# A hybrid decoder layer on one core: three adaLN sections summed on VectorE instead of in TensorE blocks, HGRN2's key copies put later, and the last down tile in two column halves

## The chip, the cores and the metric

The kernel runs on one core of a Trainium2 chip. The metric is the device time of one execution in microseconds (us). The engines are named as in the profile: PE is TensorE's matrix multiplication and PEld its weight load, DVE is VectorE, ACT is ScalarE, POOL is GpSimd, SP is SyncE, which issues nearly all DMAs of this kernel. `L12` is line 12 of the kernel before.

## What is computed

One layer: 512 tokens of width 1024, everything in fp32. A small vector `c` gives, through a weight matrix `w_ada` of 1024 x 6144, six modulation vectors ("adaLN sections") of width 1024 each: shift, scale and gate for the first sub-layer (sections 0 to 2) and for the second (3 to 5). Cut to what matters here:

```python
cs = silu(c)                                  # (1, 1024)
mod = cs @ w_ada + b_ada                      # (1, 6 * 1024)
sh1, sc1, gt1, sh2, sc2, gt2 = split(mod, 6)

h  = rmsnorm(x, norm1_g) * (1 + sc1) + sh1
z  = h @ w_in                                 # split into the inputs of two head groups
o  = concat(hgrn2(...), nsa(...))             # gated linear recurrence | sparse attention
x  = x + gt1 * (o @ w_out)

h2 = rmsnorm(x, norm2_g) * (1 + sc2) + sh2
u  = causal_dwconv(h2 @ w_up)                 # width 3
a, v = split(u, 2)
x  = x + gt2 * ((silu(a) * v) @ w_down)       # w_down is 2816 x 1024
```

`hgrn2` is a recurrence over four heads of width 128 with gates between 0 and 1; `nsa` has eight query heads of width 64 and three branches (compressed, selected, window).

## The kernel before

**Tiles.** Tokens are cut into four row tiles of 128. The large products (`w_in`, `w_out`, `w_up`, `w_down`) are made of three fp32r matmuls each (`mm3`, L137 to L139): every operand is split into a high part (ACT cast, L133) and a remainder (DVE subtraction, L134). Weights come by DMA into `raw` (two buffers, issued by `issue`, L206 to L211), are split into `whi` and `wlo` and used one part ahead (`piece`, `next_parts`).

**Order.** The order of instructions on each engine is the order in which the code writes them. Where several pieces of work run side by side, they are generators, and `emit` (L147) takes turns: it always advances the one that has gone the smallest share of its given number of yields. So the number beside a generator sets how it is spread. The stages in order are:

1. adaLN sections 0 and 1 and the first projection (to about 60 us);
2. `proj_kv` beside `prep(PREP1)`, then `proj_a` beside `prep(PREP2)`: projections on PE, norms and rotary embedding of queries and keys on DVE and ACT;
3. two `proj_T` stages beside `PREP3` and `PREP4`; the second also starts `attention`;
4. three `emit` calls with the hidden layers of the compression (`cmp_hidden`, `cmp_out`), attention, a projection and `hg_levels` of the first pair of HGRN2 heads; then a long `emit` of what is left of attention (82 yields), the dense projections (29) and `hg_levels` of both pairs (19 and 40);
5. `hg_mix`, `hg_flip`, the output projection `out_mm`, the second norm;
6. the up projection with convolution, in 44 steps, and the down projection.

**Attention** (L1060): in step s the scores of unit s go to PE and their row maxima to DVE (L981); the transposes of unit s - 4 to PE (L1029, `LAG` = 4) with their copy on ACT (L1036); the exponentials of s to ACT (L998); the weights of s - 1 to DVE and ACT; one step after the transposes come the products with the values (L1057).

**HGRN2 levels** (`hg_levels`, L1104): seven levels per pair of heads. In each, PE multiplies copied keys `E` with queries (L1131), DVE updates the keys in place (L1132, L1135), `early_keys` has ACT copy the keys for the next level (`hgE`, L1100), and after a yield DVE merges the product (L1140) and updates the queries (L1143). Then come a third block and two more yields.

**adaLN sections 3, 4 and 2** (L1249 to L1318) are computed beside stage 4. Each section is cut in four quarters of 256 columns. `ada_load` fetches one quarter of all 1024 rows of `w_ada` (1 MB) into the single buffer `aw`; `ada_quarter` multiplies it by `cs32`, the vector repeated in 32 columns, in eight fp32 matmuls of 32 output rows (L1268), then issues the next load. The profile shows each such matmul as two records. The sums over four groups of rows stand in four groups of partitions.

- For sections 3 and 4 (`ada_cols`) ACT copies each quarter to `arow` (L1296); a section is written to HBM (L1299), read back as columns by `cols_load` (L1308) after stage 4, turned by PE (L1313), summed over the four groups and completed by DVE (L1315 to L1318): `sh2` and `a2`.
- For section 2 (`ada_rows`) each quarter is split by ACT and DVE (L1281, L1282), spread to all partitions by two matmuls with a matrix of ones (L1285, L1286), and added to `gt1`, which holds the bias (L1287).

`adas`, the chain of these generators, is not a partner in `emit`: `attention` advances it after every two or four of its units (`next(beside, None)`).

**The down projection** (the end of the file): for each half of 512 output columns, four accumulators `dn` (one per row tile) collect 22 blocks of 128 rows, two blocks per step. In the last step of a half the row tiles are finished one after the other; each is then multiplied by `gt2` (L1614), added to `x1` (L1615) and stored (L1616).

Buffers that matter: `aw` (one of 8 KB per partition), the pool `g` of 32 buffers of 4 KB per partition (`G`), eight 512-wide temporaries and four of 256 (`TMP`), and eight PSUM banks (`PS`).

Of the kernel before, what the change touches and what calls it, by code (L numbers as in the profile page):

```python
# [54 lines left out]
QUICK = 7  # L55
LEVELS = (1, 2, 4, 8, 16, 32, 64)
# [36 lines left out]
def hybrid_layer_kernel(ctx: ExitStack, tc: tile.TileContext, d: dict, out: bass.AP, dbg=None):  # L93
# [287 lines left out]
    def ada_row(k):  # L381
# [205 lines left out]
    ada_row(0)  # L587
# [14 lines left out]
    for k in range(KT):  # L602
        h = hT[k]
        n = k + 1
        if n < KT:
            if k + 3 < KT:
                if k == 0:
                    load_small()
                load_ada()
                load_qf()  # L610
                if k == 4:
                    sp.dma_start(cb[:, C_LMASK:], d["consts"][:, C_LMASK:])
            elif k + 3 == KT:
                issue()
            if n in ROWS:
                ada_row(n)
            wn = first_weights(n)
            wfn = first_gates(n)
# [4 lines left out]
        if k == 0:  # L623
            for e, f in ((0, 0), (0, 1), (1, 0)):
# [3 lines left out]
                if e + f == 0:  # L628
                    ada_row(1)
# [430 lines left out]
    def attention(beside):  # L1060
# [5 lines left out]
        for s in range(n + LAG + 1):  # L1066
# [10 lines left out]
            v = s - LAG - 1  # L1077
# [26 lines left out]
    def hg_levels(pr, res):  # L1104
# [17 lines left out]
        while L < P:  # L1122
# [14 lines left out]
            if 2 * L < P:  # L1137
# [10 lines left out]
            tot = nt  # L1148
            L *= 2
# [102 lines left out]
    order = [(s, q) for s in (3, 4, 2) for q in range(4)]  # L1252
    aws = []

    def ada_load(s, q):
        raw = wp.tile([P, KT, 256], F32, tag="aw", name=nm("aw"), bufs=1)
        sp.dma_start(raw, ada_view[:, :, s * D + q * 256:s * D + q * 256 + 256])
        aws.append(raw)

    def ada_quarter():  # L1260

        raw = aws.pop()
        ps = PS("rows")
        for j in range(KT):
            g = 32 * (j % 4)
            pe.matmul(ps[g:g + 32, 0:256], cs32[:, j], raw[:, j], start=(j < 4), stop=(j >= 4),  # L1268
                      skip_group_check=True)
        if order:  # L1270
            ada_load(*order.pop(0))
        return ps[:, 0:256]

    def ada_rows(s, res):

        for q in range(4):
            sums = ada_quarter()
            sl = slice(q * 256, q * 256 + 256)
            hl = TMP([P, 2, 256], F32R, tag="rhl")
            hi, lo = hl[:, 0], hl[:, 1]  # L1280
            sc.activation(hi, sums, AF.Copy, scale=1.0 / 32)  # L1281
            ve.scalar_tensor_tensor(lo, sums, 1.0 / 32, f32(hi), ALU.mult, ALU.subtract)  # L1282
            yield
            ps = PS()
            pe.matmul(ps[:, 0:256], onesr, hi, start=True, stop=False)  # L1285
            pe.matmul(ps[:, 0:256], onesr, lo, start=False, stop=True)  # L1286
            ve.tensor_tensor(res[:, sl], ps[:, 0:256], res[:, sl], ALU.add)  # L1287
            yield

    def ada_cols(s, dst, bias, gain=None):  # L1290


        rows = G([D], s="arow")
        for q in range(4):
            sums = ada_quarter()
            sc.copy(rows[:, q * 256:q * 256 + 256], sums)  # L1296
            yield
            if q == 3:
                sp.dma_start(adr[4 * len(late_cols):4 * len(late_cols) + 4], rows[0:P:32])  # L1299
                late_cols.append((dst, bias, gain))  # L1300
            yield

    adr = hbm.tile([8, D], F32, name="adr")
    late_cols = []

    def cols_load():
        r = TMP([64, P], tag="acol")
        sp.dma_start(r, adr.rearrange("g (k p) -> (g k) p", p=P))  # L1308
        return r

    def cols_sum(r):
        ps = PS()
        pe.transpose(ps[:, 0:64], r, ident[0:64, 0:64])  # L1313
        for n, (dst, bias, gain) in enumerate(late_cols):
            ve.tensor_reduce(dst, ps[:, 32 * n:32 * n + 32].rearrange("p (g k) -> p k g", g=4), AX.X, ALU.add)  # L1315
            ve.tensor_tensor(dst, dst, bias, ALU.add)
            if gain is not None:
                ve.tensor_tensor(dst, dst, gain, ALU.mult)  # L1318
# [53 lines left out]
    adas = chain(ada_cols(3, sh2, vt[:, 24:32]), ada_cols(4, a2, bsc2, vt[:, 56:64]), ada_rows(2, gt1))  # L1372
# [21 lines left out]
    ada_load(*order.pop(0))  # L1394
# [3 lines left out]
    emit((proj_T(lambda j, a: hg_query(0, j, a)), 8), (prep(PREP3), len(PREP3)))  # L1398
    emit((proj_T(lambda j, a: hg_forget(1, j, a)), 8), (prep(PREP4), len(PREP4)), (part(attn, 10), 10))
# [4 lines left out]
         (part(lev0, 10), 10))  # L1404
    emit((chain(part(hv0, 4), cmp_hidden(2), cmp_hidden(3)), 8), (part(attn, 6), 6), (part(lev0, 6), 6))
    dense = chain(hv0, hg_value_odd(), proj_T(hg_gate_out(0)), proj_T(hg_gate_out(1), False), late())
    emit((cmp_out(), 4), (part(dense, 4), 4), (part(attn, 4), 4), (part(lev0, 4), 4))
    emit((attn, AN), (dense, DN), (lev0, L0N), (lev1, L1N))
    for _ in adas:
        pass  # L1410
    acol = cols_load()
# [83 lines left out]
    out_mm(1, 0, KN)  # L1495
    hg_mix(2)
# [95 lines left out]
    steps = []  # L1592
    for half in range(2):
        for k0 in range(0, NFF, 4):
            for a in range(0, min(4, NFF - k0), 2):
                steps.append((half, k0, a))
    up_post(nst - 2)
# [40 lines left out]
```

## Time and profile before

| | |
|---|---|
| median of 3 runs | 722.96 us (722.7 to 723.0) |
| the profiled execution | 723.01 us |
| its span, first to last instruction | 721.2 us |
| TensorE clock granted | 1.000 |
| PE, DVE, ACT, POOL busy | 711.8, 433.6, 325.8, 107.3 us |
| first and last adaLN matmul of sections 3, 4, 2 (L1268) | 135.8 and 294.6 us |
| loads of `aw` for them | 12 of 1 MB, issued from 94.8 to 285.4 us |

How to read the views: the page gives busy time by engine and the chain of work that ended last, followed back from the last instruction. A group of instructions is one line: source line, engine, operation, what it writes and reads, the shape and the count; then the busy time in us and the mean of one in ns; then how long the engine stood before them, and who ended that. The timeline gives start and duration in us. A wait line names who waited for whom: us in total, times, the longest. A matmul's duration contains its way through the array, so the distance from start to start is what one costs in a row of them.

### The profile page before, as it was taken

The numbers are of one execution on the slowest core, as the hardware profiler recorded it, in microseconds if no ns is written. First come the engines' busy times: TensorE is split into PE (matmuls) and PEld (weight loads), VectorE is DVE, ScalarE is ACT, GpSimd is POOL, SyncE is SP. The second block draws the span as 40 slices with busy tenths as digits, with TensorE's granted clock in tenths as the row PEclk, the third lists the DMA queues.
The fourth block names the chain that finished last, engine by engine and source line by source line (L and its number), as shares of the span: only waits on it lengthen the run. The fifth ranks groups of instructions, "written<-read, shape, count | busy, mean of one in ns | idle before, by whom it ended". The sixth has DMA issues, their size and how long they took to land.

```text
span 721.2 us, 10429 instructions
## 1 busy us (share of the span) xinstructions
PE 711.8 (99%) x4080; PEld 580.3 (80%) x4080; DVE 433.6 (60%) x828; ACT 325.8 (45%) x626; POOL 107.3 (15%) x99
## 2 busy tenths in 40 slices
PE   8999999999999999999999999999999999999997
PEld 4668898788887777888898888888888888888885
DVE  5688587855767765768845666665555554224223
ACT  5555446655557566424644344444434433211210
POOL 1005020200000000010007627521101101000000
PEclk9999999999999999999999999999999999999999
DMA  9994171465233312724225444543343332225301
GB/s 287 289 269 132 35 231 59 127 206 153 101 119 118 118 59 90 256 68 122 58 60 151 142 116 134 159 116 87 89 118 88 88 117 77 99 88 174 116 31 58
DMA packets 109413, 90.25 MB, mean 125 GB/s; under 512 B 5579, under 2 KB 95275, under 8 KB 109365
## 3 DMA queue, kind: packets, MB, share of 16 engines
q1 hardware_dynamic: 109109, 89.49, 40.8%
q8 instruction: 32, 0.52, 0.3%
q10 hardware_dynamic: 256, 0.11, 0.1%
q14 instruction: 16, 0.13, 0.1%
HBM read 87.46 MB, written 2.13 MB: 124 GB/s over the span
## 4 chain that ended last, share of the span: by engine, by line
PE 88%; DVE 5%; DMA 2%; SPq 2%; ACT 1%; issue 1%; POOL 0%; ACTq 0%; DVEq 0%; POOLq 0%
PE u L138 11%; PE u L139 11%; PE u L137 11%; PE dn L138 6%; PE dn L137 6%; PE dn L139 6%; PE pT L137 3%; PE pT L139 3%; PE pT L138 3%; PE oT L1057 3%; PE F L1029 3%; PE S L977 2%; PE lev L1131 2%; PE oh L137 2%; PE oh L139 2%; PE oh L138 2%
## 5 line engine op out<-in xcount | busy, mean ns | idle before, releaser
L134 DVE TENSOR_TENSOR wlo<-raw,whi 128x1024 fp32r<-128x1024 f32 (+1 forms) x87 | 111.4, 1281 | 145.7 <-ACT whi L133 145.2
L137 PE MATMUL u<-h2h,whi 128*128 128x512 f32 (+1 forms) x360 | 136.7, 380 | 0.0
L138 PE MATMUL u<-h2l,whi 128*128 128x512 f32 (+1 forms) x360 | 136.7, 380 | 0.0
L139 PE MATMUL u<-h2h,wlo 128*128 128x512 f32 (+1 forms) x360 | 136.6, 380 | 0.0
L133 ACT CAST whi<-raw 128x1024 fp32r<-128x1024 f32 (+1 forms) x87 | 89.7, 1031 | 95.0 <-PE dn L139 80.0
L137 PEld LDWEIGHTS u<-h2h,whi 128*128 128x128 f32 x360 | 67.7, 188 | 12.9
L139 PEld LDWEIGHTS u<-h2h,wlo 128*128 128x128 f32 x360 | 67.7, 188 | 12.7
L138 PEld LDWEIGHTS u<-h2l,whi 128*128 128x128 f32 x360 | 67.7, 188 | 12.7
L138 PE MATMUL dn<-wlo,gT 128*128 128x512 f32 x160 | 62.3, 390 | 0.0
L139 PE MATMUL dn<-whi,gT 128*128 128x512 f32 x160 | 62.3, 389 | 0.0
L137 PE MATMUL dn<-whi,gT 128*128 128x512 f32 x160 | 62.2, 389 | 0.0
L1544 POOL TENSOR_TENSOR y<-y,y 128x512 f32<-128x512 f32 x22 | 28.3, 1288 | 165.0 <-DVE y L1539 165.0
L360 POOL TENSOR_TENSOR hrs<-hrs,mhalf 128x4 f32<-128x4 f32 (+2 forms) x16 | 17.7, 1124 | 223.5 <-DVE hrs L359 223.5
L133 ACT CAST gT<-y 128x512 fp32r<-128x512 f32 x20 | 12.4, 621 | 71.6 <-POOL y L1544 71.6
L998 ACT ACTIVATE pt<-S,mx 128x128 f32<-128x128 f32 (+3 forms) x64 | 33.8, 534 | 17.6 <-DVE mx L981 15.1
L137 PE MATMUL pT<-hT,whi 128*128 128x512 f32 x96 | 41.3, 430 | 0.0
L134 DVE TENSOR_TENSOR gT<-y,gT 128x512 fp32r<-128x512 f32 x20 | 14.9, 743 | 43.3 <-ACT gT L133 43.3
L139 PE MATMUL pT<-hT,wlo 128*128 128x512 f32 x96 | 37.8, 394 | 0.0
L138 PE MATMUL pT<-hT,whi 128*128 128x512 f32 x96 | 37.5, 391 | 0.0
L981 DVE TENSOR_REDUCE mx<-S 128x1 f32<-128x384 f32 (+3 forms) x48 | 28.4, 596 | 14.6 <-PE S L979 14.6
L1542 ACT ACTIVATE y<-y 128x512 f32<-128x512 f32 x22 | 13.9, 632 | 49.6 <-DVE y L1539 49.6
L138 PEld LDWEIGHTS dn<-wlo,gT 128*128 128x128 f32 x160 | 30.0, 188 | 6.4 <-DVE wlo L134 0.2
(346 smaller groups left out, 1437.9 us busy)
## 6 DMA issues: line engine op xcount, KB each, us to landing
raw<-in_w_up SPq DMA_DIRECT2D x44, 512.0 KB, 4.1
aw<-in_w_ada SPq DMA_DIRECT2D x12, 1024.0 KB
raw<-in_w_down SPq DMA_DIRECT2D x10, 1024.0 KB, 4.9
ada<-in_w_ada SPq DMA_DIRECT2D x32, 256.0 KB, 5.6
raw<-in_w_in SPq DMA_DIRECT2D x7, 1024.0 KB, 5.2
x<-in_x SPq DMA_DIRECT2D x8, 512.0 KB, 5.2
raw<-in_w_cmp SPq DMA_DIRECT2D x8, 512.0 KB
raw<-in_w_out SPq DMA_DIRECT2D x4, 1024.0 KB, 8.6
```

The lines of the kernel that those rows point to most:

```text
L133: sc.copy(hi, src)
L134: (eng or ve).tensor_tensor(lo, src, f32(hi), ALU.subtract)
L137: pe.matmul(o, ah, bh, start=start, stop=False, skip_group_check=True)
L138: pe.matmul(o, ah, bl, start=False, stop=False, skip_group_check=True)
L139: pe.matmul(o, al, bh, start=False, stop=stop, skip_group_check=True)
L360: gp.tensor_tensor(o, o, mhalf[:, 0:n], ALU.pow)
L977: pe.matmul(o, QS[i][:, h], KK[g, 0][:, 0:i + 1, bsl], start=True, stop=False)
L981: ve.tensor_reduce(mx[:, 0:n], ps[:, 0:n * W].rearrange("p (b w) -> p b w", b=n), AX.X, ALU.max, negate=True)
L998: sc.activation(pt[:, sl], ps[:, sl], AF.Exp, bias=mx[:, e:e + 1], accum_out=su[:, h % 2, e:e + 1])
L1029: pe.transpose(ps[:, j * P:(j + 1) * P], src[:, j * P:(j + 1) * P], ident)
L1057: pe.matmul(oTs[i][r:r + 64, h // 2], VV[:, j, b, g], src[:, q * P:(q + 1) * P], start=(h == 0 and b == 0 and j == 0), stop=False, skip_gr ...
L1544: gp.tensor_tensor(ys[0], ys[0], y, ALU.mult)
```

## The change

There are three parts.

**The sums.** `w_ada` is no longer fetched by column quarters but by row tiles: one load is 128 rows by all 1024 columns of a section (512 KB), 24 loads in all, into the two halves of `aw` in turn. `ada_sums` multiplies each row tile by its column of `cs` and adds it up in `aacc` on DVE, in halves of 512 columns, two yields per row tile; the load for the row tile after the next is issued after the second. It is a partner in `emit`: 8 yields beside `proj_kv`, 4 beside `proj_a`, 4, 4 and 2 in the three stages of the compression, 26 in the long one. What stands in a section's `aacc` has then to be summed over the 128 partitions. For sections 3 and 4 that is one block of four 32-column matmuls by ones (`ada_row`), one ACT copy and one write to HBM, at the moment when `attention` next advances `adas`; reading back takes 16 rows instead of 64, and the sums of four groups fall away. For section 2 it is two splits of 512 columns and four matmuls by ones (`ada_gate`), placed around `hg_mix(0)` and before `hg_mix(2)`.

**The key copies.** `early_keys` is called after the merge and the query update of its level, one yield later than before (`EPOS` = 1).

**The last down tile.** In the second half of columns the last four blocks of rows are taken together: row tiles 0 and 1, then 2, and then row tile 3 in two halves of 256 columns, the second in an accumulator of its own (`tail`). The older sum for that part is multiplied by `gt2` and added to `x1` ahead of time (`rest`). The last operations of the kernel are then 256 columns wide.

The constants `VLAG` and `ADL` are 1; with `VLAG` = 1 the order in `attention` is as before. `ada_row` of the first stage is only renamed. The diff, cut to its core:

```diff
+EPOS = 1
+VLAG = 1
+ADL = 1
+ADAS = (3, 4, 2)
+ADW = 512
+AD0, AD1, AD2, AD3, AD4, AD5, AD6 = 8, 4, 0, 0, 4, 4, 2
+ADN = 26
...
-            if 2 * L < P:
+            if 2 * L < P and EPOS == 0:
                 E = early_keys(KS, 2 * L)
             yield
...
+            if 2 * L < P and EPOS == 1:
+                E = early_keys(KS, 2 * L)
             yield
...
-    order = [(s, q) for s in (3, 4, 2) for q in range(4)]
+    ada_rows = [(s, k) for s in ADAS for k in range(KT)]
...
+    def ada_load():
+        if len(aws) < len(ada_rows):
+            if not aws:
+                aw_[0] = wp.tile([P, 2, D], F32, tag="aw", name=nm("aw"), bufs=1)
+            s, k = ada_rows[len(aws)]
+            raw = aw_[0][:, len(aws) % 2]
+            sp.dma_start(raw, ada_view[:, k, s * D:(s + 1) * D])
+            aws.append(raw)
...
+    def ada_sums():
+        for n, (s, k) in enumerate(ada_rows):
+            if k == 0:
+                aacc[s] = G([D], s="aacc")
+            for c in range(0, D, ADW):
+                o, w = aacc[s][:, c:c + ADW], aws[n][:, c:c + ADW]
+                if k:
+                    ve.scalar_tensor_tensor(o, w, cs[:, k:k + 1], o, ALU.mult, ALU.add)
+                else:
+                    ve.tensor_scalar(o, w, cs[:, 0:1], None, ALU.mult)
+                if c + ADW == D and k == KT - 1:
+                    summed.append(s)
+                yield
+                if c + ADW == D:
+                    ada_load()
+
+    def ada_row(s):
+        acc = aacc.pop(s)
         ps = PS("rows")
...
+        for g in range(4):
+            pe.matmul(ps[32 * g:32 * g + 32, 0:256], ones[:, 0:32], acc[:, 256 * g:256 * g + 256], start=True,
+                      stop=True, skip_group_check=True)
+        row = TMP([P, 256], tag="arow")
+        sc.copy(row, ps[:, 0:256])
+        sp.dma_start(adr[s - 3].rearrange("(g c) -> g c", g=4), row[0:P:32])
+
+    def ada_gate(s, res):
+        acc = aacc.pop(s)
+        hls = []
+        for c in range(0, D, 512):
+            hls.append([TMP([P, 512], F32R, tag=t) for t in ("rhi", "rlo")])
+            split(*hls[-1], acc[:, c:c + 512])
+            yield
+        for c in range(0, D, 512):
             ps = PS()
+            for n, t in enumerate(hls.pop(0)):
+                pe.matmul(ps, onesr, t, start=(n == 0), stop=(n == 1))
+            ve.tensor_tensor(res[:, c:c + 512], ps, res[:, c:c + 512], ALU.add)
+            yield
+
+    def ada_out():
+        for s in ADAS:
+            while s not in summed:
+                yield
+            for _ in range(ADL):
+                yield
+            if s > 2:
+                ada_row(s)
+                yield
...
-    emit((kv, KVN), (prep(PREP1), len(PREP1)))
-    emit((proj_a(), 8), (prep(PREP2), len(PREP2)))
-    ada_load(*order.pop(0))
+    for _ in range(2):
+        ada_load()
+    emit((kv, KVN), (prep(PREP1), len(PREP1)), (part(adss, AD0), AD0))
+    emit((proj_a(), 8), (prep(PREP2), len(PREP2)), (part(adss, AD1), AD1))
...
-    emit((attn, AN), (dense, DN), (lev0, L0N), (lev1, L1N))
+    emit((attn, AN), (dense, DN), (lev0, L0N), (lev1, L1N), (adss, ADN))
...
+    next(gate1)
     hg_mix(0)
+    next(gate1)
     out_mm(0, 0, KN)
     cols_sum(acol)
     hg_mix(1)
     hg_flip(0)
     out_mm(1, 0, KN)
+    for _ in gate1:
+        pass
     hg_mix(2)
...
+    ws = [next_parts(a == 0) for a in range(2)]
+    for i, a in ((0, 0), (1, 0), (0, 1), (1, 1), (2, 0), (2, 1)):
+        for b in range(2):
+            dn_mm(i, NFF - 4 + 2 * a + b, ws[a], slice(0, 512), False, a + b == 2)
+        if a:
+            dn_out(i, 1, 0, 512)
+        elif i == 0:
+            rest = dn_sum(accs[3], x1[3][:, 768:1024], 1, 256, 512)
+    tail = PS("dnt")
+    for c, acc in ((0, None), (256, tail)):
+        for j in range(4):
+            dn_mm(3, NFF - 4 + j, ws[j // 2], slice(c, c + 256), acc is tail and j == 0, j == 3, acc)
+        dn_out(3, 1, c, c + 256, acc, rest)
```

More of the change, by code (lines that the diff above doesn't have):

```diff
@@ L1274, in ada_rows @@
[L1274 to L1282, printed above, removed]
+    aacc = {}
+    summed = []
+    def ada_load():
[6 more added lines that the diff above has]
+            aws.append(raw)
@@ L1312, in cols_sum @@
         ps = PS()
[L1313 to L1318, printed above, removed]
+        pe.transpose(ps[:, 0:16], r, ident[0:16, 0:16])
+        ve.tensor_tensor(sh2, ps[:, 0:8], vt[:, 24:32], ALU.add)
+        ve.tensor_tensor(a2, ps[:, 8:16], bsc2, ALU.add)
+        ve.tensor_tensor(a2, a2, vt[:, 56:64], ALU.mult)
     def ada_last(s, res):
```

112 lines of the change are left out of this document (46 added, 66 removed).

## The prediction

> **What bounds the kernel now.** I read the page first, its engine totals, and then the chain that ended last.
>
> ```profile
> span 721.2 us, 10429 instructions
> PE 711.8 (99%) x4080; PEld 580.3 (80%) x4080; DVE 433.6 (60%) x828; ACT 325.8 (45%) x626; POOL 107.3 (15%) x99
> ...
> PE 88%; DVE 5%; DMA 2%; SPq 2%; ACT 1%; issue 1%; POOL 0%; ACTq 0%; DVEq 0%; POOLq 0%
> ```
>
> TensorE (PE) is busy 99% of the span and holds 88% of the chain; VectorE (DVE) has 40% free. An average hides stages, so the next view is the busy time by stretch, cut where the code changes stage: key/value projection and its preparation (60 to 88), the stretch from the first adaLN block to the end of the mixed attention and HGRN2 stage (127 to 296), and, to see how much VectorE can carry, 99 to 113 and 330 to 357. Columns are us, then busy us (and instructions) of PE, PEld, DVE, ACT, POOL.
>
> ```profile
> 60.00:88.00 28.00, 27.71 (x144) 23.57 (x143) 18.11 (x37) 13.12 (x22) 5.97 (x4) 1.00 0.16 44
> 99.00:113.00 14.00, 14.00 (x72) 11.63 (x71) 11.70 (x38) 6.45 (x19) 2.06 (x3) 1.00 0.46 144
> 127.00:296.00 169.00, 168.79 (x1394) 133.08 (x1394) 117.01 (x276) 102.04 (x260) 4.00 (x5) 1.00 0.40 126
> 330.00:357.00 27.00, 27.00 (x144) 22.96 (x143) 23.12 (x50) 13.43 (x34) 1.64 (x3) 1.00 0.44 116
> ```
>
> In the 169 us that hold all twelve adaLN blocks, PE stands 0.2 us and DVE works 117.01 us, a share of 0.69. DVE shares of 0.836 (11.70 of 14) and 0.856 (23.12 of 27) occur elsewhere with PE never idle. So here PE is the bound, and work taken from it should be won, as long as VectorE can take what it is given.
>
> **The blocks that go.** The groups of instructions by line give their size, the timeline their place.
>
> ```profile
> L1268 PE MATMUL rows<-aw,cs 128*32 128x256 f32 x192 | 12.9, 385 | 0.0
> L1282 DVE SCALAR_TENSOR_TENSOR rhl<-rows,rhl 128x256 fp32r<-128x256 f32 x4 | 1.7, 424 | 4.1 <-ACT rhl L1281 4.1
> L1287 DVE TENSOR_TENSOR gt<-ps,gt 128x256 f32<-128x256 f32 x3 | 1.3, 419 | 0.5 <-PE ps L1286 0.5
> ...
> 135.80 1.07 PE L1268 MATMUL rows<-aw,cs 128*32 128x256 f32 x16
> 136.80 0.38 PE L977 MATMUL S<-KK,qs 128*128 128x256 f32 x1
> ...
> 264.91 0.36 PE L1285 MATMUL ps<-rhl,onesr 128*128 128x256 f32 x1
> 265.32 1.97 PE L1057 MATMUL oT<-pT,VV 128*64 128x128 f32 x32
> ```
>
> Each of the twelve quarters puts 16 records between its neighbours and holds PE 1.00 us (135.80 to 136.80): 12.0 us at least, 12.9 by the group's busy time, which I take. The four pairs for gt1 hold PE 265.32 - 264.91 = 0.41 us each, 1.6 us. **Removed from PE: 14.5 us.**
>
> What PE gets back is two short blocks and the two column halves of gt1. A block (`ada_row`) has four 32-column matmuls instead of eight: half of 1.07, say 0.55, between 0.5 and a full 1.07; two make 1.1. The gate now has four matmuls 512 wide; such a one follows its neighbour by 0.23 us (715.75 to 715.98 below), so 0.92, and they stand behind 296. **PE net: -14.5 + 1.1 + 0.92 = -12.5 us.**
>
> **What VectorE takes on.** 24 rows of `w_ada`, each in two halves of 512 columns: the first row of each section a multiplication (6 instructions), the others a multiply-add with a column as scalar (42). This multiply-add does not occur at this width, so its neighbours bound it.
>
> ```profile
> L402 DVE SCALAR_TENSOR_TENSOR rows<-ada,cs,rows 128x256 f32<-128x256 f32 x21 | 10.2, 484 | 0.6
> L1538 DVE SCALAR_TENSOR_TENSOR y<-u,cv,y 128x511 f32<-128x511 f32 x44 | 32.7, 743 | 0.0
> L1210 DVE SCALAR_TENSOR_TENSOR hgt<-tmp,pT 128x512 f32<-128x512 f32 x4 | 2.8, 689 | 4.8 <-ACT tmp L1209 4.8
> L1422 DVE TENSOR_TENSOR tmp<-oh,gt 128x512 f32<-128x512 f32 x8 | 5.5, 685 | 0.0
> L1435 DVE TENSOR_SCALAR hx<-x,rs 128x512 f32<-128x512 f32 x8 | 3.5, 482 | 0.7 <-POOL rs L360 0.7
> ```
>
> Below stands 689 ns (constant scalar), above 2 x 484 (the same instruction, two half widths); I take 743, which has a column as scalar and nearly this width. The multiplication is L1435: 482. So 42 x 0.743 + 6 x 0.482 = 34.1 us, by stage: 5.4 in the key/value projection (8 instructions), 3.0 in the next (4), and 25.7 from 127 on (36, four of them multiplications: 32 x 0.743 + 4 x 0.482).
>
> The Trainium skill ("VectorE: DVE Perf Modes", the section on the TRN2 errata) gives a two-input fp32 operation (N + 151)/0.96 ns, an estimated 691 ns at 512; the plain L1422 with 685 agrees, L1538 with 743 does not. By the page the added work would be 2.2 us smaller.
>
> From 127 on DVE then has 117.0 - 1.7 - 1.3 + 25.7 = 139.7 us of work, and PE 169 - 14.5 + 1.1 = 155.6 us: **a share of 0.90**, more than any stretch above shows. DVE runs its instructions in order: behind each added one wait the row maxima of the scores, the key updates of HGRN2 and the split of the next weights; behind these ScalarE's exponentials and PE's transposes. The scores are transposed four steps later, which hides a delay of some us, not a lasting one. The most exposed place is here:
>
> ```profile
> 186.97 0.44 DVE sc L952
> ...
> 194.72 0.66 PE F L1029 x4
> ```
>
> In the chain that ended last, between these two pieces lie 13 more of VectorE and two of ScalarE, and none of PE: it runs through VectorE here already. Two added instructions fall into it: 1.5 us of stall. For the rest of the stretch I take as much again. Together 3.1 us, which is DVE at a share of 0.88 (139.7/0.88 = 158.7). Full cover would give 0; the highest share shown, 0.856, gives 163.2, or 7.6 us.
>
> **The first stages** lose no PE work, so there the additions can only cost. PE's waits and SyncE's DMAs there:
>
> ```profile
> PE ps L762 <- DVE xr L696: 0.3, 1, 0.3
> ...
> 56.26 0.47 SPq L1371 DMA_DIRECT2D gt<-in_b_ada  x1
> 63.76 30.96 SPq L211 DMA_DIRECT2D raw<-in_w_in  x6
> ...
> 65.23 0.69 DVE L696 TENSOR_TENSOR xr<-accq,hrs 128x512 f32<-128x512 f32 x1
> ...
> 67.97 0.69 DVE L134 TENSOR_TENSOR qhl<-dst,qhl 128x512 fp32r<-128x512 f32 x1 [0.69 <-ACT qhl L133]
> 70.07 0.68 DVE L696 TENSOR_TENSOR xr<-accq,hrs 128x512 f32<-128x512 f32 x1
> ```
>
> PE already waits 0.3 us for the second L696. Ahead of it fall two multiplications, 0.96 us; one lies in the 0.69 us wait at 67.97. I take **+0.5 us**, between 0 and 1. Later ones fall into DVE's 9.9 idle us up to 88. The two row loads pass SyncE after 56.73, ahead of its next weight load at 63.76, and are wanted at about 65.4.
>
> **Row loads.** 12 loads of 1 MB become 24 of 512 KB, still through SyncE's queue, and each waits for DVE's last use of its half buffer. It is issued two of the yields of `ada_sums` before its row is used.
>
> ```profile
> raw<-in_w_up SPq DMA_DIRECT2D x44, 512.0 KB, 4.1
> ...
> out_x<-tmp SPq DMA_DIRECT2D x8, 256.0 KB, 2.0
> ```
>
> Landing takes about 4.1 us; the last 26 yields spread over the final `emit`, which by the code fills about the last 110 us up to 296, so two of them are some 8 us. Cost 0; if that cover went, DVE and everything behind it would stand until the row is there.
>
> **The key copies.** ScalarE's copy of HGRN2's keys goes one yield later, past the rest of that yield's work.
>
> ```profile
> ACT hgE L1100 <- DVE hgK L1135: 14.0, 8, 2.6
> ...
> PEld ps L1241 <- DVE on L1233: 0.5, 1, 0.5
> ```
>
> ScalarE stands 14.0 us waiting for the keys, but at 102 of 169 us it is no bound, and PE takes the copy only at the next level, two yields on. I count 0, between -1 and +1.
>
> **Behind 296** DVE loses small sums and gains four 512-wide operations (2.8 us), two of them ahead of `hg_mix(2)`. There the chain of `hg_mix(3)` ends in PE's wait on L1233. The first two fit where the old gate addition stood; the last two push the reduction by about 1.2 us, of which PE's own 0.92 counts already: **+0.3 us**, between 0 and 1.4.
>
> **The tail.** The end of the timeline, a stretch with 256-wide matmuls, and the groups that prepare and load weights:
>
> ```profile
> 715.75 0.39 PE L137 MATMUL dn<-whi,ghi 128*128 128x512 f32 x1
> 715.98 0.39 PE L138 MATMUL dn<-wlo,ghi 128*128 128x512 f32 x1
> 716.63 0.69 DVE L1614 TENSOR_TENSOR tmp<-dn,gt 128x512 f32<-128x512 f32 x1
> 717.36 0.69 DVE L1615 TENSOR_TENSOR tmp<-tmp,x 128x512 f32<-128x512 f32 x1
> ...
> 356.10 0.28 PE L138 MATMUL u<-h2l,whi 128*128 128x256 f32 x1
> 356.22 0.28 PE L139 MATMUL u<-h2h,wlo 128*128 128x256 f32 x1
> ...
> L134 DVE TENSOR_TENSOR wlo<-raw,whi 128x1024 fp32r<-128x1024 f32 (+1 forms) x87 | 111.4, 1281 | 145.7 <-ACT whi L133 145.2
> L133 ACT CAST whi<-raw 128x1024 fp32r<-128x1024 f32 (+1 forms) x87 | 89.7, 1031 | 95.0 <-PE dn L139 80.0
> L137 PEld LDWEIGHTS u<-h2h,whi 128*128 128x128 f32 x360 | 67.7, 188 | 12.9
> ```
>
> The last two operations shrink to 256 columns (0.42 as L1287): -0.54. 24 matmuls at 0.12 instead of 12 at 0.23 cost +0.12, and the last store is half as big. **-0.4 us**, between -0.8 and 0. The second pair of weight parts is now needed after 12 matmuls of 0.23, 2.8 us; cast and split take 1.0 + 1.3, so it is just there, and 0.5 us is lost if it is late.
>
> **The sum.** -12.5 + 3.1 + 0.5 + 0 + 0.3 - 0.4 = -9.0. The profiled execution took 723.01 us (span 721.2, 1.8 around it), the median of the three runs is 722.96: no difference to carry over. 723.0 - 9.0 = **714.0 us**.
>
> **The rivals.**
> 1. *VectorE hides it all.* Nothing stalls: -12.5 - 0.4 + 0.3, **710.4 us**. For it: PE idles 0.2 us in 169 today. Against: a share of 0.90.
> 2. *VectorE becomes the bound, slower.* Place: 127 to 296. If DVE, with its in-order waits, holds no more than 0.82, the stretch lasts 170.4 us, 1.4 more than now, and with 0.92 + 0.5 + 0.3 - 0.4 the kernel takes **725.7 us**. It decides at 139.7/(169 - 1.3) = 0.833. Against: 0.836 and 0.856 were carried without a stall of PE, so they are no ceiling.
> 3. *PE was not full, nothing won.* Its busy time is modelled; if the blocks lay in hidden waits, the other work closes up only to what VectorE lets through, near **723 us**. The starts 0.23 us apart speak against it. The Trainium skill ("Trainium Kernel Development and Optimization", Performance Expectations) calls matmul busy time a bad measure and the share of weight loads a good one; by it 133.08 of 169, 79%, would leave a fifth unproven. A load takes 188 ns of the 0.23 us pitch (last row of the fence above), so 81% is already full, and the trace does not bear the rule out here.
> 4. *The rows land late.* If each of the 13 rows in the last block came 1 us late, DVE would stand 13 us: **727 us**. Against: 8 us of lead.
>
> **Chances.** Forecast (DVE at 0.86 to 0.895, 711.5 to 718.5) 0.64; rival 1 0.16; rival 2 0.09; rival 3 0.05; rival 4 0.06. A measurement of this kernel can tell about 0.2% from no change, 1.4 us. Faster 0.64 + 0.16 = 0.80, same 0.05, slower 0.15. The range 710.0 to 719.0 takes in the forecast, rival 1 and both ends of the small terms.
>
> **What would show it.** No L1268; `ada_row` twice at half a us; the multiply-adds at 0.69 to 0.75 us; the stretch up to the end of attention about 10 us shorter, with DVE at 0.86 to 0.90 of it; PE idle or stretched a few us, most around 185 to 195, released by DVE; SyncE ahead of DVE with the rows. I am wrong if DVE waits for `aw` landings, if the multiply-add takes well over 0.75 us, or if the stretch shrinks less than 5 us.

## The result, and the profile after

The changed kernel takes 714.84 us (median of 4 runs, 714.64 to 715.1) against 722.98 us for the kernel before, measured beside it (722.7 to 723.5): a ratio of 0.9888 [0.9874, 0.9903], 8.1 us less. The profiled execution took 714.7 us and its span is 712.9 us, 8.3 us shorter than before. Line numbers from here on are those of the changed kernel. The page's opening, its engine totals and its chain by engine:

```profile
span 712.9 us, 10152 instructions
...
PE 700.6 (98%) x3912; PEld 575.9 (81%) x3912; DVE 462.7 (65%) x874; ACT 323.7 (45%) x618; POOL 108.0 (15%) x99
...
PE 72%; DVE 18%; ACT 4%; DMA 2%; SPq 2%; issue 1%; POOL 1%; ACTq 0%; POOLq 0%; DVEq 0%
```

PE has 11.2 us less work (711.8 before), DVE 29.1 us more (433.6). PE is still the bound, but DVE's part of the chain has grown from 5% to 18%. The groups of the changed kernel show the new work:

```profile
L1287 DVE SCALAR_TENSOR_TENSOR aacc<-aw,cs,aacc 128x512 f32<-128x512 f32 x42 | 31.1, 746 | 0.0
...
L1302 PE MATMUL rows<-aacc,ones 128*32 128x256 f32 x16 | 1.3, 391 | 0.0
...
L1289 DVE TENSOR_SCALAR aacc<-aw,cs 128x512 f32<-128x512 f32 x6 | 2.9, 478 | 0.0
```

The 42 multiply-adds take 746 ns each, and "idle before" is 0.0 for them: not one waited for its row to land.

**Where the time went.** The first and last starts of a tile cut the kernel into stages. `hgo` begins when attention and the HGRN2 levels end, `u` with the up projection. Before, then after:

```profile
L1222 PE MATMUL hgo<-hv,hgA x32: 270/275/377, 299.2 to 314.6; 128*128 128x128 f32 x32
...
L137 PE MATMUL u<-h2h,whi x360: 283/389/396, 354.5 to 596.0; 128*128 128x512 f32 x164, 128*128 128x256 f32 x16
```

```profile
L1233 PE MATMUL hgo<-hv,hgA x32: 270/275/377, 289.3 to 307.3; 128*128 128x128 f32 x32
...
L144 PE MATMUL u<-h2h,whi x360: 283/389/396, 347.1 to 588.6; 128*128 128x512 f32 x164, 128*128 128x256 f32 x16
```

With the starts of `kva` (60.5 before, 60.2 after) and `dn` (596.7 and 589.3), found in the same way:

| stage | before | after | difference | predicted |
|---|---|---|---|---|
| up to `kva` | 60.5 | 60.2 | -0.3 | 0 |
| `kva` to `hgo` | 238.7 | 229.1 | -9.6 | -9.8 |
| `hgo` to `u` | 55.3 | 57.8 | +2.5 | +1.2 |
| `u` to `dn` | 242.2 | 242.2 | 0 | 0 |
| `dn` to the end | 124.5 | 123.6 | -0.9 | -0.4 |

The whole gain arises between `kva` and `hgo`, and 2.5 us are given back right behind it. One execution is not exact to half a us: up to `kva`, where the kernel before and its two variants further down (only the copies, only the last tile) have the same code, they take 60.5, 60.2 and 60.8 us. The prediction's own terms for the two rows are -14.5 + 1.1 + 3.1 + 0.5 and 0.92 + 0.3.

The busy time by stretch (us; PE, PEld, DVE, ACT, POOL; granted clock, DMA share, GB/s), before and then after. The stretch 127 to 289 lies inside attention in both:

```profile
127.00:289.00 162.00, 161.84 (x1314) 127.20 (x1314) 111.85 (x259) 98.11 (x253) 4.00 (x5) 1.00 0.39 123
```

```profile
127.00:289.00 162.00, 159.17 (x1249) 129.87 (x1249) 136.31 (x308) 101.43 (x254) 4.03 (x5) 1.00 0.36 113
127.00:150.00 23.00, 22.18 (x141) 16.56 (x141) 20.30 (x41) 13.72 (x48) 4.03 (x5) 1.00 0.52 162
...
210.00:230.00 20.00, 18.95 (x144) 15.19 (x142) 17.39 (x41) 14.15 (x37) 0.00 (x0) 1.00 0.33 104
230.00:260.00 30.00, 29.78 (x220) 23.17 (x221) 26.84 (x63) 17.93 (x42) 0.00 (x0) 1.00 0.23 73
...
60.00:88.00 28.00, 27.36 (x142) 23.30 (x141) 22.75 (x45) 12.83 (x22) 5.85 (x4) 1.00 0.50 150
```

DVE carries a share of 0.84 (136.31 of 162) instead of 0.69. PE now stands 2.8 us of the 162, before 0.2. Two narrow stretches hold most of it: 0.8 us in 127 to 150, where DVE's share is 0.88, and 1.05 us in 210 to 230, where it is 0.87. But in 230 to 260 the share is 0.89 and PE stands only 0.2 us, so the share alone does not set the loss. PE's waits from 55 to 330 name what it stood for:

```profile
PE F L1036 <- ACT pt L1025: 1.1, 3, 0.6
PE oh L145 <- DVE wol L141: 1.1, 1, 1.1
PE lev L1138 <- DVE hgQ L1122: 0.8, 1, 0.8
PE F L1036 <- DVE pt L1027: 0.7, 1, 0.7
PE ps L769 <- DVE xr L703: 0.6, 1, 0.6
```

Three belong to attention and the levels; the last was 0.3 before and is the price in the first projection (in 60 to 88 PE is busy 27.36 us, before 27.71). The second, `wol`, lies behind attention. The timeline there:

```profile
289.77 0.75 DVE L1287 SCALAR_TENSOR_TENSOR aacc<-aw,cs,aacc 128x512 f32<-128x512 f32 x1
...
290.43 2.35 DVE L141 TENSOR_TENSOR wol<-raw,woh 128x1024 fp32r<-128x1024 f32 x2
...
291.71 0.50 PE L145 MATMUL oh<-wol,mixN 128*128 128x512 f32 x1 [1.10 <-DVE wol L141]
```

The last multiply-add ends at 290.5. Only then can DVE split the first weights of the output projection, and PE stands 1.1 us for them: attention has ended on PE before DVE is done with its share.

### The profile page after: what moved, and what is told of

It is laid out like the page before. It is cut to its first block, busy times and chain, and to the rows that moved or that the text cites. A ratio compares the mean times of both kernels' runs of the same rounds, so it can differ in the third digit from the quotient of the medians.

```text
span 712.9 us, 10152 instructions
## 1 busy us (share of the span) xinstructions
PE 700.6 (98%) x3912; PEld 575.9 (81%) x3912; DVE 462.7 (65%) x874; ACT 323.7 (45%) x618; POOL 108.0 (15%) x99
## 4 chain that ended last, share of the span: by engine, by line
PE 72%; DVE 18%; ACT 4%; DMA 2%; SPq 2%; issue 1%; POOL 1%; ACTq 0%; POOLq 0%; DVEq 0%
PE u L145 11%; PE u L146 11%; PE u L144 11%; PE dn L145 6%; PE dn L146 6%; PE dn L144 6%; DVE mx L988 2%; DVE aacc L1287 2%; DVE wlo L141 1%; PE oh L144 1%; PE oh L146 1%; PE oh L145 1%; DVE rows L409 1%; PE pT L144 1%; PE pT L146 1%; PE pT L145 1%
## 5 line engine op out<-in xcount | busy, mean ns | idle before, releaser
L145 PE MATMUL dn<-wlo,gT 128*128 128x512 f32 (+1 forms) x160 | 62.1, 388 | 0.0
L146 PE MATMUL dn<-whi,gT 128*128 128x512 f32 (+1 forms) x160 | 62.1, 388 | 0.0
L144 PE MATMUL dn<-whi,gT 128*128 128x512 f32 (+1 forms) x160 | 62.1, 388 | 0.0
L140 ACT CAST gT<-y 128x512 fp32r<-128x512 f32 x20 | 12.4, 621 | 70.9 <-POOL y L1579 70.9
L144 PEld LDWEIGHTS dn<-whi,gT 128*128 128x128 f32 x160 | 30.1, 188 | 6.2
```

The costliest lines, as they stand in the source:

```text
L140: sc.copy(hi, src)
L144: pe.matmul(o, ah, bh, start=start, stop=False, skip_group_check=True)
L145: pe.matmul(o, ah, bl, start=False, stop=False, skip_group_check=True)
L146: pe.matmul(o, al, bh, start=False, stop=stop, skip_group_check=True)
```

## The experiments

Each ratio is to the kernel before, run on the same chip (723.05 to 723.35 us); "against the changed kernel" compares medians with 714.84 us. In the expectations A is the account on record; the other letters are its rivals.

**The sums left out.** The 42 multiply-adds go; loads, blocks and gate stay.

```diff
-                if k:
-                    ve.scalar_tensor_tensor(o, w, cs[:, k:k + 1], o, ALU.mult, ALU.add)
-                else:
+                if k == 0:
                     ve.tensor_scalar(o, w, cs[:, 0:1], None, ALU.mult)
```

> The changed kernel without its 42 multiply-adds on VectorE: each section keeps only its first row tile's multiplication, so the modulation vectors are incomplete; the 24 loads, the two short blocks, the gate and everything else stay. Theory A (PE is the bound, and what the added VectorE work costs is PE waiting for late VectorE results: some 3 us up to the end of attention, a few tenths in the first stages and 1 to 1.5 us behind attention): 4 to 5 us faster than the changed kernel, 709.5 to 711 us. Rival B (VectorE's work is hidden, and what is missing of the removed 14.5 us was never PE time): within 1 us of the changed kernel, 714 to 715.

Measured: 710.29 us, 0.9820 [0.9807, 0.9833]. Its landmarks:

```profile
L1233 PE MATMUL hgo<-hv,hgA x32: 270/275/377, 286.3 to 302.6; 128*128 128x128 f32 x32
...
L144 PE MATMUL u<-h2h,whi x360: 283/389/396, 342.6 to 584.1; 128*128 128x512 f32 x164, 128*128 128x256 f32 x16
```

With `kva` at 60.8, the stage from `kva` to `hgo` lasts 225.5 us, 13.2 less than before; the prediction had PE win 14.5 - 1.1 = 13.4. The sums cost 229.1 - 225.5 = 3.6 us in this stage, the predicted 3.1 + 0.5. The agreement is rough: the six multiplications are still there, and in this run PE also waits 0.8 us for weights of the compression (`raw` from `w_cmp`), which it does not in the changed kernel. From `hgo` to `u` it takes 56.3 us: 1.0 more than before, which is put down to the gate (0.92 predicted), and the other 1.5 us of the changed kernel's 57.8 go with the sums. The time is in A's range.

**The blocks put back.** Beside the sums, twelve blocks of eight 32-column matmuls on data that is there anyway, at the places where attention advances `adas`.

```diff
+    def with_blocks():
+        for n in range(24):
+            if n % 2 == 0:
+                ps = PS("rows")
+                for j in range(KT):
+                    g = 32 * (j % 4)
+                    pe.matmul(ps[g:g + 32, 0:256], cs32[:, j], cb[:, 0:256], start=(j < 4), stop=(j >= 4),
+                              skip_group_check=True)
+            next(adas, None)
+            yield
...
-    attn = attention(adas)
+    attn = attention(with_blocks())
```

> The changed kernel with twelve blocks of eight 32-column matmuls put back on PE at the places where attention advances the adaLN work; their results are not used. Theory A (PE is the bound, with a few us of waits for VectorE that such blocks can fill): 9 to 13 us slower than the changed kernel, 724 to 728 us. Rival C (with the sums VectorE has become the bound of the stretch, so that PE has room): less than 4 us slower, under 719.

Measured: 722.8 us, 0.9992 [0.9983, 1.0001], 8.0 us over the changed kernel. The same stretch:

```profile
127.00:289.00 162.00, 162.00 (x1325) 127.27 (x1326) 129.82 (x288) 96.56 (x244) 4.03 (x5) 1.00 0.34 105
```

PE stands 0.0 us: the blocks first fill the waits that the sums make, and the rest of them lengthens the kernel. From `kva` to `hgo` they cost 9.3 us (238.4 against 229.1), about what 12.0 us of blocks less 2.8 us of waits leave. Behind it 1.5 us come back (56.3): the wait for `wol` is gone, since DVE has longer to finish. The 8.0 us lie below the 9 to 13 that A gave, which had not counted what comes back, and far above the less than 4 us of the rival by which DVE had become the bound and PE had room.

**The key copies where they were.**

```diff
-EPOS = 1
+EPOS = 0
```

> The changed kernel with the key copies at their old place (EPOS = 0), nothing else. The prediction's own count: no difference within 1 us, since ScalarE is no bound and PE takes the copies only at the next level. Rival D (ScalarE's stands for the keys, 14.0 us before and 0.6 us after, now delay the exponentials, since VectorE writes the keys later): 1 to 3 us slower than the changed kernel.

Measured: 717.92 us, 0.9930 [0.9917, 0.9944], 3.1 us over the changed kernel; in the trace 2.6 us of it lie between `kva` and `hgo` (231.7 against 229.1). The prediction's count, no difference within 1 us, is out; the rival's cause is what the trace shows. The group of the copies in the kernel before, in the changed one and in this one:

```profile
L1100 ACT COPY hgE<-hgK 128x512 f32<-128x512 f32 x14 | 8.9, 634 | 14.2 <-DVE hgK L1135 14.0
```

```profile
L1107 ACT COPY hgE<-hgK 128x512 f32<-128x512 f32 x14 | 8.9, 637 | 0.6 <-DVE hgK L1142 0.6
```

```profile
L1107 ACT COPY hgE<-hgK 128x512 f32<-128x512 f32 x14 | 8.8, 630 | 18.8 <-DVE hgK L1142 18.8
```

Put early, the copy stands at the head of ACT's queue and waits for DVE's key update, 14.0 us in the kernel before and 18.8 us beside the sums. Behind it wait the copies of the transposes, and PE for them:

```profile
PE S L984 <- ACT pT L1043: 1.6, 1, 1.6
PE oT L1064 <- ACT pT L1043: 1.3, 1, 1.3
```

One yield later the wait is 0.6 us.

**The copies alone,** in the kernel before:

```diff
-            if 2 * L < P:
-                E = early_keys(KS, 2 * L)
             yield
...
+            if 2 * L < P:
+                E = early_keys(KS, 2 * L)
             yield
```

> The kernel before with the key copies put later and nothing else. If the copies matter only where VectorE is late (as the run with the copies early suggests), no difference within 0.5 us; if ScalarE's 14.0 us of standing cost the kernel before as well, 1 to 3 us faster than the kernel before.

Measured: 722.35 us, 0.9987 [0.9979, 0.9996]: 1.0 us, at the foot of the second case; 0.8 us of it lie between `kva` and `hgo` (237.9 against 238.7). The same edit is worth 1.0 us where DVE has 31% free and 3.1 us where it has 16%.

**The copies another yield later.**

```diff
-EPOS = 1
+EPOS = 2
```

> The changed kernel with the key copies one more yield later (EPOS = 2). If what the later copies gained (3.1 us in the changed kernel) came from ScalarE no longer standing for the keys, which it does for 0.6 us now, nothing is left to gain: within 0.5 us, or slower by up to 2 us if PE then waits for the copies at the next level.

Measured: 716.57 us, 0.9906 [0.9891, 0.9921]; the interval overlaps the changed kernel's. Now PE itself waits for the copy:

```profile
PE lev L1138 <- ACT hgE L1107: 0.8, 2, 0.5
```

One yield has the lowest median of the three places; that it is better than two is not shown.

**The last tile alone,** in the kernel before: only the new end of the down projection (`dn_mm`, `dn_sum`, `dn_out`, `tail`, as in the diff above).

> The kernel before with the new order of the last down tile alone. The prediction counted -0.4 us between -0.8 and 0 for it; the traces of before and of the changed kernel differ by 0.9 us from the first down matmul to the end. Expected 0.4 to 1 us faster than the kernel before; the rival, that the second pair of weight parts comes late, gives no difference.

Measured: 722.78 us, 0.9993 [0.9984, 1.0002]. Its 0.6 us can't be told from zero by time; the trace has `dn` to the end 0.7 us shorter (124.5 to 123.8). The last matmul of the kernel before, and how the changed kernel ends:

```profile
716.21 0.39 PE L139 MATMUL dn<-whi,glo 128*128 128x512 f32 x1
```

```profile
709.10 0.28 PE L146 MATMUL dnt<-whi,glo 128*128 128x256 f32 x1
709.42 0.42 DVE L1636 TENSOR_TENSOR tmp<-dnt,gt 128x256 f32<-128x256 f32 x1 [0.55 <-PE dnt L146]
709.88 0.42 DVE L1637 TENSOR_TENSOR tmp<-tmp,tmp 128x256 f32<-128x256 f32 x1
```

The last matmul starts 3.8 us ahead of the end (712.9 - 709.10), before 5.0 (721.2 - 716.21).

**The gate behind the mix.** All of `ada_gate` moved behind `hg_flip(3)`, to see whether it is what costs between `hgo` and `u`.

```diff
-    next(gate1)
     hg_mix(0)
-    next(gate1)
...
-    for _ in gate1:
-        pass
...
     hg_flip(3)
+    for _ in gate1:
+        pass
     out_weights("on", 1, 4)
```

> The changed kernel with all of the gate of section 2 (two splits, four matmuls, two additions) moved behind hg_flip(3), where its result is first needed soon after. Theory A (the first split and the two additions delay the reductions of hg_mix, and PE waits for the last of them): 0.5 to 1.2 us faster than the changed kernel. Rival E (what is lost behind attention is the backlog that VectorE brings from the sums, not the gate): no difference within 0.4 us.

Measured: 721.4 us, 0.9971 [0.9960, 0.9982], 6.6 us slower than the changed kernel; neither theory had this. PE's waits:

```profile
PE ps L1319 <- ACT rhi L140: 3.5, 1, 3.5
...
PE oh L145 <- DVE wol L141: 1.1, 1, 1.1
...
PE ps L1319 <- DVE rlo L141: 0.3, 1, 0.3
```

The wait for `wol` stands as it was, so the gate does not cause it; that DVE's remainder of sums does is shown by the next run. At its new place the gate's casts lie behind those of `hg_flip` on ACT, and its matmuls stand 3.5 us at the head of PE's queue. Right behind that stand the granted clock (third number from the end of a line) is lower:

```profile
318.00:321.00 3.00, 2.63 (x6) 1.90 (x7) 2.63 (x5) 3.00 (x5) 0.00 (x0) 0.66 0.00 0
321.00:325.00 4.00, 4.00 (x16) 3.15 (x15) 4.00 (x5) 1.32 (x2) 0.00 (x0) 0.83 0.06 17
```

Matmuls of 512 columns start up to 0.43 us apart there (319.80 to 320.23), where they otherwise follow by 0.23. The ten from 318.06 to 322.62 take 4.56 us instead of 2.3, 0.3 of it the second wait. With the 3.5 us ahead of them that is about the 5.6 us by which `hgo` to `u` is longer (63.4 against 57.8). In the trace, 7.0 us longer in all, the other 1.4 lie ahead of `kva`, where the edit changes nothing. Ahead of `hg_mix(2)`, in the changed kernel, the same four matmuls take 0.23 us each:

```profile
299.97 0.39 PE L1319 MATMUL ps<-rhi,onesr 128*128 128x512 f32 x1
300.20 0.39 PE L1319 MATMUL ps<-rlo,onesr 128*128 128x512 f32 x1
...
300.88 0.38 PE L1233 MATMUL hgo<-hv,hgA 128*128 128x128 f32 x2
```

**The sums done earlier within attention:** the last 26 halves are spread over the first 26/30 of the long stage, so that none is left at its end.

```diff
-ADN = 26
+ADN = 30
```

> The changed kernel with the last 26 halves of the sums spread over the first 26/30 of the long stage (ADN = 30) instead of all of it. Theory A' (VectorE's backlog at the end of attention makes PE wait for the first output weights, 1.1 us): that wait goes, 0.5 to 1 us faster than the changed kernel. Rival G (the same work packed more densely makes PE wait earlier by as much or more): no gain or up to 1.5 us slower.

Measured: 714.97 us, 0.9883 [0.9868, 0.9898], no difference, as the rival had it. The wait for `wol` is gone and `hgo` to `u` takes 56.3 us, 1.5 less; but `kva` to `hgo` takes 230.1, 1.0 more. So the 1.5 us behind attention are the sums', and most of them come back as waits inside attention when the sums are packed more densely there.

**More of the sums ahead of attention.** Two more yields beside `proj_a` and four beside the last `proj_T`; then in a second kernel six beside the last `proj_T`.

```diff
-AD0, AD1, AD2, AD3, AD4, AD5, AD6 = 8, 4, 0, 0, 4, 4, 2
-ADN = 26
+AD0, AD1, AD2, AD3, AD4, AD5, AD6 = 8, 6, 0, 4, 4, 4, 2
+ADN = 20
```

> The changed kernel with six of the 26 halves of the long stage moved ahead: two more beside proj_a (6 instead of 4), four beside the second proj_T stage (instead of none), 20 in the long stage. Theory A (a late VectorE makes PE wait in the long stage, and the earlier stages still have VectorE time free): the long stage loses 4.5 us of VectorE work; at the average price that the run without the sums showed, 4.5 us for 31 us of work, that is 0.6 us, 1 to 1.5 if the last instructions cost more than the average; 713.3 to 714.3 us. Rival H (the earlier stages are as full): no gain or up to 1.5 us slower.

Measured: 714.42 us, 0.9880 [0.9866, 0.9893], 0.4 us under the changed kernel, which is not shown to be a gain and lies just outside A's range. In the stretch that the prediction took as proof that a DVE share of 0.836 costs nothing, PE now loses 0.4 us. The changed kernel, then this one:

```profile
99.00:113.00 14.00, 14.00 (x72) 11.45 (x71) 12.03 (x38) 6.02 (x16) 1.41 (x3) 1.00 0.34 112
```

```profile
99.00:113.00 14.00, 13.61 (x69) 10.55 (x68) 12.06 (x36) 6.02 (x16) 1.89 (x3) 1.00 0.69 225
```

DVE's share there is 0.86 in both (12.03 and 12.06 of 14), with and without a loss. So the share alone does not decide it. The wait that the trace names is 0.3 us for `wlo`, the remainder of a weight, which DVE brought late.

Then six yields beside the last `proj_T`:

```diff
-AD0, AD1, AD2, AD3, AD4, AD5, AD6 = 8, 4, 0, 0, 4, 4, 2
-ADN = 26
+AD0, AD1, AD2, AD3, AD4, AD5, AD6 = 8, 4, 0, 6, 4, 4, 2
+ADN = 20
```

> The changed kernel with all six of the moved halves beside the second proj_T stage (6 instead of none), none added beside proj_a, 20 in the long stage. The stretch from 113 to 127 us has VectorE busy for 10.6 of 14 us, and in the run with sums earlier it took four halves with PE full; the two beside proj_a were followed by 0.4 us of PE's standing between 99 and 113. Theory A: the gain of the run with sums earlier (0.4 us) without that loss, 713.8 to 714.4 us. Rival I (six do not fit there, or the sums moved out of the long stage are not what PE waits for): 714.6 or more.

Measured: 714.14 us, 0.9872 [0.9855, 0.9888], in A's range: the lowest median of all complete versions, 0.7 us under the changed kernel, but its interval overlaps the changed kernel's, so that it is better is not shown.

**All sums behind 127.** The 12 halves of the first stages moved into the full stretch: 10 x 0.746 + 2 x 0.478 = 8.4 us more work for DVE there.

```diff
-AD0, AD1, AD2, AD3, AD4, AD5, AD6 = 8, 4, 0, 0, 4, 4, 2
-ADN = 26
+AD0, AD1, AD2, AD3, AD4, AD5, AD6 = 0, 0, 0, 0, 6, 6, 4
+ADN = 32
```

> The changed kernel with no sums in the projections of keys, values and gates: the 12 halves go to the compression stages (6, 6 and 4 instead of 4, 4 and 2) and to the long stage (32 instead of 26). Theory A: VectorE's work behind 127 us grows by 8.4 us; if it is near its limit there, PE waits for most of it: 4 to 8 us slower than the changed kernel, 719 to 723 us. If VectorE still had room (rival B): within 1.5 us, 714 to 716.

Measured: 722.5 us, 0.9987 [0.9978, 0.9996], 7.7 us over the changed kernel, nearly all of its gain, and in A's range. The profiled execution took 721.38 us with a granted clock of 1.000; its span is 6.7 us longer than the changed kernel's (719.6 against 712.9). The median is that of an execution with a clock of 0.998, which no trace shows. A stretch, and PE's two longest waits:

```profile
127.00:289.00 162.00, 154.22 (x1183) 124.93 (x1184) 137.42 (x303) 96.74 (x246) 4.04 (x5) 1.00 0.40 122
...
PE F L1036 <- ACT pt L1025: 3.0, 2, 1.5
PE cps L899 <- DMA raw<-in_w_cmp: 2.4, 2, 1.6
```

DVE takes 137.42 us in the window, 1.1 more than in the changed kernel, though it has 8.4 more to do; the rest is done later, at a share of 0.85. The stage from `kva` to `hgo` grows by 5.2 us (234.3 against 229.1) and the next by 0.6. Of these 5.8 us PE stands 2.4 for weights of the compression (`raw` from `w_cmp`), whose loads come behind the row loads in SyncE's queue. So some 3.4 us are left as DVE's own price for 8.4 us of work, 0.4 us for each us added, where the 42 multiply-adds as a whole cost 4.5 us for 31.1, about 0.15 for each.

**Half the sums on GpSimd.** The right 512 columns of row tiles 6 to 23 as a multiplication and an addition on POOL:

```diff
-                if k:
+                if c and n >= 6:
+                    sv = cs[:, k:k + 1].to_broadcast([P, ADW])
+                    gp.tensor_tensor(w if k else o, w, sv, ALU.mult)
+                    if k:
+                        gp.tensor_tensor(o, o, w, ALU.add)
+                elif k:
                     ve.scalar_tensor_tensor(o, w, cs[:, k:k + 1], o, ALU.mult, ALU.add)
```

> The changed kernel with the right-hand 512 columns of row tiles 6 to 23 multiplied and added on GpSimd (two operations each) instead of VectorE: 18 of the 48 added VectorE instructions go, 13 us of its work from the compression stages on. Theory A (what is lost is PE waiting for late VectorE results): 2 to 4 us faster than the changed kernel, 711 to 713 us, with little backlog at the end of attention. Rival F (GpSimd at about 2.5 us per half is late itself, or slows VectorE through shared memory access): no gain, or slower, 714 us and more.

Measured: 717.13 us, 0.9918 [0.9904, 0.9931], 2.3 us slower than the changed kernel although 16 x 0.746 + 2 x 0.478 = 12.9 us of work were taken off DVE; so the rival. By the engine totals DVE got no relief: it is busy 462.5 us, in the changed kernel 462.7. Groups of DVE in 127 to 289 of the changed kernel, and then of this one (with one of POOL):

```profile
L141 DVE TENSOR_TENSOR wlo<-raw,whi 128x1024 fp32r<-128x1024 f32 x9 | 11.5, 1280 | 6.8 <-ACT whi L140 6.8
...
L988 DVE TENSOR_REDUCE mx<-S 128x1 f32<-128x512 f32 x16 | 10.9, 685 | 1.2 <-PE S L986 1.2
```

```profile
L141 DVE TENSOR_TENSOR wlo<-raw,whi 128x1024 fp32r<-128x1024 f32 x9 | 13.1, 1452 | 9.4 <-ACT whi L140 9.4
...
L988 DVE TENSOR_REDUCE mx<-S 128x1 f32<-128x512 f32 x16 | 10.7, 681 | 1.5 <-PE S L986 1.5
...
L1290 POOL TENSOR_TENSOR aacc<-aacc,aw 128x512 f32<-128x512 f32 x16 | 23.1, 1442 | 1.3
```

A mean hides how this happens. For a short instruction the shortest, median and longest in the same window (ns) are, in the changed kernel and then here:

```profile
L1020 DVE TENSOR_TENSOR su<-su,gates x23: 160/161/166, 130.1 to 283.2; 128x2 f32<-128x2 f32 x16, 128x4 f32<-128x4 f32 x7
```

```profile
L1020 DVE TENSOR_TENSOR su<-su,gates x23: 160/164/901, 130.3 to 287.9; 128x2 f32<-128x2 f32 x16, 128x4 f32<-128x4 f32 x7
```

Most stay as they were, and single ones get longer by up to 0.74 us. The maximum of the scores, which reads PSUM, does not change. Not every group with two operands in SBUF grew (the key updates of L1142 took 421 and 416 ns). Over all groups of DVE with the same count in both traces, mean times count grows by 9.6 us, most of the 12.9 taken off. How much of the 2.3 us this explains was not separated from the delay of the sums themselves. The profiled execution is also the longest of the four, 718.37 us, so its groups are read here and not its length.

## Why the prediction was right, and where two errors cancelled

**PE was the bound, and its term held.** Leaving the sums out gives 13.2 us in the stage against 13.4 predicted; putting the blocks back costs 8.0 us. That nothing would be won, the third rival, is out. The copies are part of the 13.2 us: if they are worth the 0.8 us that they gave in this stage alone, 12.4 are left for PE's terms. In that run PE also waits 0.8 us for weights and 0.3 us longer for `xr`, and with these it comes to 13.5. So the term holds, to within about a us. The Trainium skill ("Trainium Kernel Development and Optimization", Performance Expectations) calls matmul busy time a bad metric for how close a kernel is to roofline; the 8.0 us of the blocks put back speak against that doubt in this case.

**The multiply-adds** took 746 ns (743 taken), the 16 records of `ada_row` two blocks of about 0.57 us (0.55), the four matmuls of the gate 0.91 us (0.92). In the first stages, put at +0.5, PE loses 0.35 us (27.71 - 27.36).

**The stall of the sums** in the stage came out as predicted, 3.6 us, but from two errors, and that they cancel so closely is luck. The step that failed is *key copies 0, between -1 and +1*: the prediction took them to be worth at most 1 us, because ACT is no bound, and they are worth 3.1 us beside the sums, because a copy that waits on ACT holds up the copies of the transposes behind it, and these hold up PE. With the copies early the stage lasts 231.7 us, 6.4 over the 225.3 (238.7 - 13.4) that PE's own terms would leave. So the stall by itself was put too low, and the copies were put too low by nearly as much. The full cover of the first rival, 710.4 us, is what the kernel without sums measures (710.29); the sums cost 4.5 us in all.

**Behind 296** the step had +0.3 us beside the gate's 0.92. It came to 1.5, and the reason given, the gate's additions ahead of the reductions of `hg_mix`, is not what the waits show: DVE ends the sums after PE has ended attention, and PE stands 1.1 us for `wol`. That DVE would be behind PE was foreseen; this cause and this place, past the end of the stage, were not. DVE's share in the stretch is 0.84 and not 0.86 to 0.90: by 289 it had done 136 of the 139.7 us that the prediction put there.

**Where PE would stand.** Predicted most around 185 to 195. In the 20 us from 190 it lost 0.55 us, and more in 127 to 150 and 210 to 230. The chain of waits did run through DVE at that place, with two added instructions in it as foreseen, but PE lost less there than the 1.5 us that they were put at.

**The tail** brought 0.7 us alone and 0.9 in the changed kernel by the trace, against 0.4 (0 to 0.8); the time alone does not show it.

**The slower rival** priced DVE as the bound from a share of 0.833 on. The share of 0.84 was carried with a gain of 8.1 us, so the bound is not that low. All sums behind 127 (8.4 us more there) cost 7.7 us, of which the trace leaves some 3.4 as DVE's, so the price rises, but no share was found at which it becomes full. That rows land late, the fourth rival, is out: no multiply-add stood for one.

**Open** is what a run could not separate: how much of the 2.3 us on GpSimd is its effect on DVE, how much of the 7.7 us with all sums behind 127 is DVE's and how much the weight loads', and whether the version with six yields beside the last `proj_T` is really faster.

## What to carry to other kernels

Work taken from a full engine is won in large part even when it goes to a helper that is thereby 84% busy: by the prediction's count 12.5 us net were taken from PE, and the time fell by 8.1, with the copies and the last tile in it. The next few us on that helper cost more than the first (about 0.4 us for each us of work against 0.15), so use the time that it has free in earlier stages. When a helper fills up, look at the third engine's queue: a copy issued before its input is ready blocks everything behind it, and moving it one step later can be worth several times as much as it was before the change. A stage may look finished while its helper is behind: read the first wait after it. And a sum that comes out to the tenth can hold two errors: test each term by itself.

## What the runs showed of the hardware

With GpSimd at work beside it, single instructions of VectorE with two operands from SBUF took much longer: of 23 short ones the median was 164 ns (161 without), the longest 901 (166). Nine subtractions of 1024 columns took 1452 ns on average instead of 1280; a reduction from PSUM was unchanged (685 and 681 ns). The Trainium skill ("SBUF — State Buffer", Who interferes with whom) says that an instruction of VectorE with two SBUF inputs contends with a GpSimd instruction that reads SBUF, because they share a port pair, and that a reduction never does. The groups shown agree on both, though some groups with two inputs did not grow. GpSimd's plain addition of 512 columns took 1442 ns, its multiplication by a column 1135 ns, where VectorE did both in one instruction of 746 ns.

Right behind a stand of PE of 3.5 us (the run with the gate late) the granted clock was 0.66 for 3 us and 0.83 for the next 4, and matmuls of 512 columns started up to 0.43 us apart instead of 0.23. That the stand is the cause is not shown.
